# Triangular inverse in a delta-rule and RWKV mixer: from a substitution on VectorE to doublings on TensorE

## The chip, the cores and the metric

The kernel runs on one NeuronCore of one Trainium2 chip, in one launch. The metric is the device time of that launch in microseconds (us), lower is better. Five engines work in parallel, each in its own program order: TensorE (PE in the profile, its weight loads PEld), VectorE (DVE), ScalarE (ACT), GpSimd (POOL) and the DMA queues that SyncE (SP) issues to.

## What is computed

Three residual blocks follow one another on 512 tokens of 1024 channels. The change lies in the third. There a gated delta rule and an RWKV-7 layer run over the tokens in four chunks of 128, for eight heads each. Inside a chunk the state update needs the solution of a unit lower triangular system, 128 by 128, for each head and chunk. The reference solves it per head and chunk; in the kernel's form it is

```
Y = ((I + L)^-1)^T        L: strictly lower triangular, 128 x 128, float32
u = Y^T r                 r: 128 tokens x 64 channels
```

The kernel computes Y for two heads and four chunks at a time, so one call of `tri_inv` inverts 8 matrices, and there are 8 calls: four for the RWKV layer (`rwkv_b`), four for the delta rule (`gdn_b`).

## The kernel before

Channels lie on partitions and tokens on the free axis, except inside the mixers, where tokens lie on partitions. All large projections are matmuls of 128 by 128 weights on 512 tokens. Each weight unit is loaded by SP, rounded to a high part on ACT (L310) and completed by a low part on DVE (L312), and `mm3` (L325 to L327) issues three matmuls for each 128 channels of contraction. The order of instructions on every engine is set by a scheduler at build time; the list `MIX3` and the offsets in `PR3` say in which order and with which priority the steps of the mixers are handed to it: `ra`, `rb`, `rd` prepare, invert and run the RWKV layer of two heads, `ga`, `gb`, `gd` the delta rule. On chip each engine takes its instructions in that fixed order and waits for semaphores.

`tri_inv` (L1740) works on the four diagonal blocks of 32 of each matrix, which lie on four groups of 32 partitions:

- ACT copies the negated blocks into `iv_lc` (L1750); DVE transposes them into `iv_ld` (L1753).
- Blocks of 16 are inverted by substitution on DVE, one row at a time, all 8 matrices and both 16-blocks together: 15 steps of a product (L1756) and a sum over it (L1757), each waiting for the one before.
- Two more transposes on DVE (L1759, L1761) give the inverse in both orientations, `iv_xc` and `iv_yc`.
- 16 to 32: 32 small matmuls of 32 by 32 (L1769), a copy to SBUF on ACT (L1771), 32 and 24 more matmuls (L1775, L1778), and two additions on DVE (L1780, L1781).
- 32 to 64 (L1790 to L1801) and 64 to 128 (L1806 to L1812) go on in the same manner on TensorE and ACT.

The matmuls of `tri_inv` write to the PSUM banks of the use `mx`, of which there are two; `rwkv_b` (L2046), `gdn_b` (L1877, L1886) use the same two.

## Time and profile before

| | us |
|---|---|
| median of 3 runs (lowest, highest) | 3515.52 (3511.62, 3516.84) |
| span of the profiled execution, first to last instruction | 3510.5 |
| PE busy in the span | 3380.7 |
| DVE busy in the span | 2413.4 |
| ACT busy in the span | 1802.1 |

The profiled execution is one execution; its own time shown is the span, 5.0 us below the median of the runs. The stage in which the 8 inversions lie goes from about 2544 us to 2998 us after the span's start. All positions below are us from the span's start. [...] A float32 matmul stands in the trace as two records, one instruction of the program.

### The profile page before, as it was taken

The numbers are of one execution on the slowest core, as the hardware profiler recorded it, in microseconds if no ns is written. First come the engines' busy times: TensorE is split into PE (matmuls) and PEld (weight loads), VectorE is DVE, ScalarE is ACT, GpSimd is POOL, SyncE is SP. The second block draws the span as 40 slices with busy tenths as digits, with TensorE's granted clock in tenths as the row PEclk, the third lists the DMA queues.
The fourth block names the chain that finished last, engine by engine and source line by source line (L and its number), as shares of the span: only waits on it lengthen the run. The fifth ranks groups of instructions, "written<-read, shape, count | busy, mean of one in ns | idle before, by whom it ended". The sixth has DMA issues, their size and how long they took to land.

```text
span 3510.5 us, 50868 instructions
## 1 busy us (share of the span) xinstructions
PE 3380.7 (96%) x20328; PEld 2686.3 (77%) x20328; DVE 2413.4 (69%) x3883; ACT 1802.1 (51%) x3000; POOL 123.6 (4%) x56
## 2 busy tenths in 40 slices
PE   7999999999799999999999999999899999999998
PEld 5888888888577777766787778888667667878887
DVE  6787767787689988466565465554757788565545
ACT  6556556466544565444455543334636556544434
POOL 0000000000132330000000000000000000000000
PEclk9999999999899999999999999999969999999999
DMA  6233323321121122333321235542201111323332
GB/s 224 88 102 95 100 91 100 106 79 55 49 72 61 66 78 95 123 108 108 93 79 58 86 120 180 186 157 96 102 21 45 34 43 37 105 88 96 96 96 84
DMA packets 109663, 325.10 MB, mean 93 GB/s; under 512 B 12721, under 2 KB 13361, under 8 KB 108786
## 3 DMA queue, kind: packets, MB, share of 16 engines
q1 hardware_dynamic: 109170, 321.06, 28.1%
q8 instruction: 160, 2.62, 0.3%
q0 software_dynamic: 256, 0.79, 0.1%
q14 instruction: 77, 0.63, 0.1%
HBM read 315.51 MB, written 6.29 MB: 92 GB/s over the span
## 4 chain that ended last, share of the span: by engine, by line
PE 78%; DVE 15%; ACT 4%; issue 2%; DMA 2%; POOL 0%; SPq 0%; DVEq 0%; ACTq 0%
PE ps_pj L326 19%; PE ps_pj L325 19%; PE ps_pj L327 19%; DVE w_lo L312 2%; DMA ada_raw<-ada_w 2%; DVE iv_m L1756 1%; PE ps_mx L1388 1%; PE ps_pj L1365 1%; PE ps_mx L2046 1%; PE ps_o L1394 1%; ACT w_hi L310 1%; DVE iv_xd L1757 1%; PE ps_ad L496 1%; PE ps_mx L326 1%; DVE cv_ul L318 1%
## 5 line engine op out<-in xcount | busy, mean ns | idle before, releaser
L325 PE MATMUL ps_pj<-hh,w_hi 128*128 128x512 f32 x2344 | 937.4, 401 | 19.8 <-ACT hh L397 18.9
L327 PE MATMUL ps_pj<-hh,w_lo 128*128 128x512 f32 x2344 | 935.0, 399 | 0.0
L326 PE MATMUL ps_pj<-hl,w_hi 128*128 128x512 f32 x2344 | 934.9, 399 | 0.0
L310 ACT CAST w_hi<-w_raw 128x1024 fp32r<-128x1024 f32 (+1 forms) x435 | 454.6, 1045 | 767.4 <-PE ps_pj L326 651.2
L312 DVE TENSOR_TENSOR w_lo<-w_raw,w_hi 128x1024 fp32r<-128x1024 f32 (+1 forms) x387 | 470.2, 1216 | 336.4 <-ACT w_hi L310 330.3
L325 PEld LDWEIGHTS ps_pj<-hh,w_hi 128*128 128x128 f32 x2344 | 445.9, 190 | 127.5 <-ACT hh L397 24.3
L326 PEld LDWEIGHTS ps_pj<-hl,w_hi 128*128 128x128 f32 x2344 | 446.0, 190 | 102.0 <-issue 12.9
L327 PEld LDWEIGHTS ps_pj<-hh,w_lo 128*128 128x128 f32 x2344 | 445.6, 190 | 101.3 <-issue 10.7
L493 DVE SCALAR_TENSOR_TENSOR ada_acc<-ada_raw,sv_t_c,ada_acc 128x512 f32<-128x512 f32 x224 | 167.4, 747 | 50.3 <-DMA ada_raw<-ada_w 48.5
L967 DVE SCALAR_TENSOR_TENSOR xT<-ps_pj,ad,xT 128x512 f32<-128x512 f32 x128 | 95.5, 749 | 153.8 <-PE ps_pj L327 153.3
L312 POOL TENSOR_TENSOR w_lo<-w_raw,w_hi 128x1024 fp32r<-128x1024 f32 x48 | 121.1, 2523 | 1175.5 <-ACT w_hi L310 1175.5
L909 DVE SCALAR_TENSOR_TENSOR ps_mx<-cv_ut,vec,ps_mx 128x448 f32<-128x448 f32 (+3 forms) x192 | 128.3, 669 | 1.9 <-PE ps_mx L327 1.0
L909 DVE SCALAR_TENSOR_TENSOR ps_ad<-cv_ut,vec,ps_ad 128x480 f32<-128x480 f32 (+2 forms) x192 | 128.5, 669 | 1.6 <-ACT ps_ad L898 0.5
L327 PE MATMUL ps_pj<-w_hi,hl 128*128 128x256 f32 x416 | 119.0, 288 | 2.5 <-DVE hl L398 2.5
L325 PE MATMUL ps_pj<-w_hi,hh 128*128 128x256 f32 x416 | 120.3, 290 | 0.8 <-ACT hh L397 0.6
L326 PE MATMUL ps_pj<-w_lo,hh 128*128 128x256 f32 x416 | 120.8, 291 | 0.0
L326 PE MATMUL ps_pj<-m_yl,w_hi 128*128 128x512 f32 x256 | 99.9, 390 | 0.0
L327 PE MATMUL ps_pj<-m_yh,w_lo 128*128 128x512 f32 x256 | 99.6, 389 | 0.0
L325 PE MATMUL ps_pj<-m_yh,w_hi 128*128 128x512 f32 x256 | 99.6, 389 | 0.0
L327 PEld LDWEIGHTS ps_pj<-w_hi,hl 128*128 128x128 f32 x416 | 80.7, 195 | 5.7 <-DVE hl L398 3.2
L325 PEld LDWEIGHTS ps_pj<-w_hi,hh 128*128 128x128 f32 x416 | 80.9, 194 | 3.6 <-ACT hh L397 1.2
L326 PEld LDWEIGHTS ps_pj<-w_lo,hh 128*128 128x128 f32 x416 | 80.8, 194 | 1.5 <-issue 0.7
(786 smaller groups left out, 6513.4 us busy)
## 6 DMA issues: line engine op xcount, KB each, us to landing
ada_raw<-ada_w SPq DMA_DIRECT2D x288, 256.0 KB, 2.8
w_raw<-w_in SPq DMA_DIRECT2D x97, 512.0 KB, 3.2
w_raw<-hgrn_w_in SPq DMA_DIRECT2D x64, 512.0 KB, 3.2
w_raw<-w_mlp SPq DMA_DIRECT2D x64, 512.0 KB, 3.3
w_raw<-conv_w_in SPq DMA_DIRECT2D x48, 512.0 KB, 3.2
w_raw<-w_ffn_in SPq DMA_DIRECT2D x44, 512.0 KB, 3.5
w_raw<-hgrn_w_v SPq DMA_DIRECT2D x16, 512.0 KB, 3.3
w_raw<-hgrn_w_out SPq DMA_DIRECT2D x16, 512.0 KB, 3.2
```

Of the source, the lines that this page charges most:

```text
L310: nc.scalar.copy(hi, raw)
L312: (nc.gpsimd if self.on_pool else nc.vector).tensor_tensor(lo, raw, hi.bitcast(F32), op=ALU.subtract)
L318: self.nc.vector.tensor_tensor(lo, src, hi.bitcast(F32), op=ALU.subtract)
L325: mm(out, wh, xh, start=first, stop=False)
L326: mm(out, wh, xl, start=False, stop=False)
L327: mm(out, wl, xh, start=False, stop=last)
L493: nc.vector.scalar_tensor_tensor(acc, raw, cond[:, k:k + 1], acc, op0=ALU.mult, op1=ALU.add)
L496: nc.tensor.matmul(col[:, b:b + 1], acc[:, 128 * b:128 * b + 128], self.c("ones")[:, 0:1], start=True, stop=True)
L909: stt(o, x, tap(j), o, op0=ALU.mult, op1=ALU.add)
L967: self.nc.vector.scalar_tensor_tensor(self.xT[:, m, :], acc, gate[:, m:m + 1], self.xT[:, m, :], op0=ALU.mult, op1=ALU.add)
L1365: mm(sc[:, :n], q[gs, 128 * i:n], ks[b][gs, 0:n], start=True, stop=True)
L1388: mm(banks[c // 512][:, c % 512:c % 512 + 128], p_[:, off[i] + 128 * s:off[i] + 128 * s + 128], dg[:, i, :], start=True, stop=True)
```

## The change

The substitution, its three transposes and the separate step from 16 to 32 go. In their place the diagonal blocks grow from 2 to 32 in four equal levels (2 to 4, 4 to 8, 8 to 16, 16 to 32). One product on DVE cuts the blocks into five masked parts, one for each level (`iv_c`, 128 x 1280); the first part plus the identity is the inverse of the blocks of 2. Each level is 32 matmuls, a copy on ACT, 64 matmuls and one addition on DVE of both orientations (`iv_xy`, 128 x 512). From 32 to 128 nothing changes. The constant `m16` becomes `mlev` and `eye32`, so one constant load grows from 128x160 to 128x320 elements. Comments are stripped from the file, which shifts line numbers; the cuts below are the code.

```diff
-    b3 = {"bones": ..., "m16": f((p % 32 < 16) & (np.arange(32)[None] >= 16))}
+    s32, t32 = p % 32, np.arange(32)[None]
+    lev = [(s32 // (2 * w) == t32 // (2 * w)) & (s32 % (2 * w) < w) & (t32 % (2 * w) >= w) for w in (1, 2, 4, 8, 16)]
+    b3 = {"bones": ..., "mlev": -f(np.concatenate(lev, axis=1)), "eye32": f(s32 == t32)}
...
         for q in q4:
-            nc.scalar.mul(lc[q, 0:8, :], LA[q, :, 0, q], -1.0)
-        ld = iv("iv_ld")
-        nc.vector.transpose(ld.rearrange("p t s -> p t s"), lc.rearrange("p h t -> p t h"))
-        for i in range(1, 16):
-            m = self.tmpd("iv_m", [P, 2, i, i])
-            tt(m, dview(ld, 32 * i, [[528, 2], [0, i], [1, i]]), dview(xd, 0, [[528, 2], [1, i], [32, i]]), op=ALU.mult)
-            nc.vector.tensor_reduce(dview(xd, 32 * i, [[528, 2], [1, i]]), m, axis=mybir.AxisListType.X, op=ALU.add)
-        nc.vector.transpose(xc.rearrange("p h j -> p j h"), xd.rearrange("p i j -> p j i"))
-        nc.vector.transpose(yc.rearrange("p h i -> p i h"), xd)
-        tt(c16, lc[:, 0:8, :], self.c("m16").unsqueeze(1).to_broadcast([P, 8, 32]), op=ALU.mult)
-        (one level: 32 matmuls, copy, 32 + 24 matmuls, two additions)
+            nc.scalar.copy(lc[q], LA[q, :, 0, q])
+        tt(cl, lc.unsqueeze(1).to_broadcast([P, 5, 8, 32]),
+           self.c("mlev").rearrange("p (l t) -> p l t", l=5).unsqueeze(2).to_broadcast([P, 5, 8, 32]), op=ALU.mult)
+        tt(xy[:, 1], cl[:, 0], b8(self.c("eye32")), op=ALU.add)
+        nc.vector.transpose(xy[:, 0].rearrange("p h t -> p (h t)"), xy[:, 1].rearrange("p h t -> p (h t)"))
+        for lev in range(1, 5):
+            ps = self.bank("mx", [P, 8, 32])
+            for hc in range(8):
+                for q in q4:
+                    mm(ps[q, hc, :], cl[q, lev, hc, :], xx[q, hc, :], start=True, stop=True)
+            b = c32("iv_b")
+            nc.scalar.copy(b, ps)
+            ps = self.bank("mx", [P, 2, 8, 32])
+            for hc in range(8):
+                for q in q4:
+                    mm(ps[q, 1, hc, :], b[q, hc, :], yy[q, hc, :], start=True, stop=True)
+                for q in q4:
+                    mm(ps[q, 0, hc, :], yy[q, hc, :], b[q, hc, :], start=True, stop=True)
+            tt(xy, xy, ps, op=ALU.add)
```

The scheduler places the rest anew around these instructions, from the first inversion on; the set of all other instructions stays. TensorE before, at the second inversion: the last projections that stand ahead of it, then its one level from 16 to 32 (L1769, L1775, L1778) and the next step (L1790).

```order
L325 MATMUL ps_pj<-hh,w_hi 128x512
L326 MATMUL ps_pj<-hl,w_hi 128x512
L327 MATMUL ps_pj<-hh,w_lo 128x512
L325 MATMUL ps_pj<-hh,w_hi 128x512
L1769 MATMUL ps_mx<-iv_xc,iv_b 32x32 x32
L326 MATMUL ps_pj<-hl,w_hi 128x512
L1819 MATMUL ps_pa<-rw_sq,cst_b_20722 128x512
L1775 MATMUL ps_mx<-iv_yc,iv_b 32x32 x32
L1778 MATMUL ps_mx<-iv_b,iv_yc 32x32 x24
L1977 MATMUL ps_pa<-s_lo,rw_lw 128x512
```

TensorE now, at the second inversion: the end of its first level's 64 matmuls (L1774 and L1776 alternate in fours, eight times), what is put in before the second level (L1768), its 32 matmuls, and what is put in before the next 64. L328 to L330 are the three matmuls of `mm3`, L2025 is the second matmul of the RWKV layer's gate.

```order
L1776 MATMUL ps_mx<-iv_b,iv_xy 32x32 x4
L2025 MATMUL ps_pa<-s_sg_20780,rw_lw 128x512
L330 MATMUL ps_pj<-hh,w_lo 128x512
L328 MATMUL ps_pj<-hh,w_hi 128x512
L329 MATMUL ps_pj<-hl,w_hi 128x512
L1768 MATMUL ps_mx<-iv_xy,iv_c 32x32 x32
L330 MATMUL ps_pj<-hh,w_lo 128x512
L328 MATMUL ps_pj<-hh,w_hi 128x512
L329 MATMUL ps_pj<-hl,w_hi 128x512
L330 MATMUL ps_pj<-hh,w_lo 128x512
L328 MATMUL ps_pj<-hh,w_hi 128x512
L1774 MATMUL ps_mx<-iv_xy,iv_b 32x32 x4
```

Between the levels stand one to five matmuls of other work in most places; the run of 17 projections that stood ahead of the second inversion before is spread over these gaps. DVE before, at the end of the second inversion's substitution: a step of it stands between two instructions of other work, and the two transposes follow.

```order
L1756 TENSOR_TENSOR iv_m<-iv_ld,iv_xd 128x450
L1493 TENSOR_TENSOR gd_gz<-gd_gz,si_e 128x512
L1757 TENSOR_REDUCE iv_xd<-iv_m 128x2x15
L1642 SCALAR_TENSOR_TENSOR rw_k<-rw_pad,s_mu_20735,rw_k 128x512
L1759 STREAM_TRANSPOSE iv_xc<-iv_xd 128x32x32
L1761 STREAM_TRANSPOSE iv_yc<-iv_xd 128x32x32
L312 TENSOR_TENSOR w_lo<-w_raw,w_hi 128x1024 x2
```

DVE now, at the second inversion: the additions that end its first two levels (L1777) and what stands between and behind them. L437, L1496 and L1853 are work of the delta rule's preparation, L315 is the low part of a weight.

```order
L1777 TENSOR_TENSOR iv_xy<-iv_xy,ps_mx 128x512
L437 SCALAR_TENSOR_TENSOR si_e<-gd_z,si_e 128x512
L1853 SCALAR_TENSOR_TENSOR gd_z<-gd_pad,vec_20708,gd_z 128x512
L1496 TENSOR_TENSOR gd_z<-gd_z,si_e 128x512
L1637 MEMSET rw_pad 128x1
L437 SCALAR_TENSOR_TENSOR si_e<-gd_z,si_e 128x512
L315 TENSOR_TENSOR w_lo<-w_raw,w_hi 128x1024
L1777 TENSOR_TENSOR iv_xy<-iv_xy,ps_mx 128x512
```

Where 15 pairs of short instructions stood, one inversion now has four additions, each behind other work in the queue.

## Rows read from the trace of the kernel before

**Rows 1.** The page: busy us of each engine, share of the span, instructions.

```profile
PE 3380.7 (96%) x20328; PEld 2686.3 (77%) x20328; DVE 2413.4 (69%) x3883; ACT 1802.1 (51%) x3000; POOL 123.6 (4%) x56
```

**Rows 2.** Busy time by stretch (start:end, length, engines), granted clock, DMA: the whole stage.

```profile
core 0: us, PE busy (x) PEld busy (x) DVE busy (x) ACT busy (x) POOL busy (x), PEclk, DMA share, GB/s
2544.00:2998.00 454.00, 427.65 (x3920) 314.04 (x3919) 344.22 (x695) 254.04 (x509) 1.61 (x3) 0.90 0.11 37
```

**Rows 3.** The stage's critical chain by line, shares of its 454 us.

```profile
by line: DVE iv_m L1756 9.2%; PE ps_mx L2046 8.1%; DVE iv_xd L1757 6.0%; PE ps_pj L327 5.2%; PE ps_pj L326 5.0%; PE ps_pj L325 4.6%; DVE w_lo L312 3.6%; PE ps_mx L1886 3.5%; DVE iv_xc L1759 3.3%; DVE iv_yc L1761 2.8%; issue 2.7%; PE ps_mx L
```

**Rows 4.** Waits of TensorE in the stage: us in total, times, longest.

```profile
PE ps_mx L1769 <- DVE iv_xc L1759: 8.7, 7, 2.3
PE ps_pa L1830 <- DVE rw_B L2013: 4.6, 1, 4.6
PE ps_mx L1778 <- issue: 2.2, 4, 0.9
```

**Rows 5.** Groups of DVE in the stage: form, count, busy us, mean ns, idle before.

```profile
L1756 DVE TENSOR_TENSOR iv_m<-iv_ld,iv_xd 128x2 f32<-128x2 f32 (+14 forms) x120 | 55.4, 461 | 1.9
L1757 DVE TENSOR_REDUCE iv_xd<-iv_m 128x2 f32<-128x2 f32 (+14 forms) x120 | 38.8, 324 | 1.8
L312 DVE TENSOR_TENSOR w_lo<-w_raw,w_hi 128x1024 fp32r<-128x1024 f32 x30 | 36.5, 1218 | 8.2 <-ACT w_hi L310 8.2
L1759 DVE STREAM_TRANSPOSE iv_xc<-iv_xd 128x1024 f32<-128x1024 f32 x8 | 16.7, 2082 | 0.0
L1753 DVE STREAM_TRANSPOSE iv_ld<-iv_lc 128x1024 f32<-128x1024 f32 x8 | 15.7, 1967 | 1.7 <-ACT iv_lc L1750 1.7
L1761 DVE STREAM_TRANSPOSE iv_yc<-iv_xd 128x1024 f32<-128x1024 f32 x8 | 15.6, 1948 | 0.0
L1780 DVE TENSOR_TENSOR iv_yy<-iv_yc,ps_mx 128x256 f32<-128x256 f32 x8 | 3.4, 420 | 0.0
L2025 DVE TENSOR_TENSOR rw_bon<-rw_v,ps_pa 128x512 f32<-128x512 f32 x4 | 2.8, 688 | 1.4 <-PE ps_pa L2024 1.4
```

**Rows 6.** TensorE at the second inversion, full clock: start, us, records, idle before.

```profile
2667.55 0.75 PE L1769 MATMUL ps_mx<-iv_xc,iv_b 32*32 32x32 f32 x64 [2.28 <-DVE iv_xc L1759]
2668.23 0.50 PE L326 MATMUL ps_pj<-hl,w_hi 128*128 128x512 f32 x1
2669.53 0.72 PE L1775 MATMUL ps_mx<-iv_yc,iv_b 32*32 32x32 f32 x62
2670.10 0.67 PE L1778 MATMUL ps_mx<-iv_b,iv_yc 32*32 32x32 f32 x46
2670.70 1.12 PE L1977 MATMUL ps_pa<-s_lo,rw_lw 64*128 64x512 f32 x2
2672.92 0.69 PE L1790 MATMUL ps_mx<-iv_xx,s 32*32 32x32 f32 x32 [0.66 <-DVE iv_xx L1781]
```

**Rows 7.** DVE just behind that level, and ACT's copy at the third inversion.

```profile
2672.04 0.41 DVE L1780 TENSOR_TENSOR iv_yy<-iv_yc,ps_mx 128x256 f32<-128x256 f32 x1
2724.67 0.37 ACT L1771 COPY iv_b<-ps_mx 128x256 f32<-128x256 f32 x1 [1.77 <-PE ps_mx L1769]
```

**Rows 8.** TensorE at the first inversion, where the clock was low.

```profile
2584.37 1.07 PE L1775 MATMUL ps_mx<-iv_yc,iv_b 32*32 32x32 f32 x64 [0.18 <-DVE iv_yc L1761]
2586.15 1.06 PE L1778 MATMUL ps_mx<-iv_b,iv_yc 32*32 32x32 f32 x47 [0.69 <-issue]
2587.14 0.80 PE L327 MATMUL ps_pj<-hh,w_lo 128*128 128x512 f32 x1
```

**Rows 9.** Busy time and clock of the stage in four stretches, columns as in rows 2.

```profile
2540.00:2565.00 25.00, 24.31 (x56) 15.48 (x57) 14.78 (x35) 6.32 (x14) 0.54 (x1) 0.50 0.07 23
2565.00:2583.00 18.00, 16.58 (x111) 11.06 (x112) 14.62 (x22) 9.75 (x14) 0.00 (x0) 0.94 0.10 36
2583.00:2642.00 59.00, 57.45 (x407) 41.62 (x396) 29.31 (x53) 21.61 (x48) 0.00 (x0) 0.54 0.06 19
2642.00:2998.00 356.00, 332.62 (x3378) 248.41 (x3378) 288.09 (x593) 219.82 (x440) 1.07 (x2) 0.99 0.13 42
```

## The prediction

> **What bounds the kernel now.** The page comes first: TensorE is busy 96% of the span, DVE 69%, ACT 51% [rows 1]. Whatever adds TensorE work that nothing hides costs time; what it takes from DVE pays only where TensorE waits for DVE. All 8 inversions lie in one stage, so the busy time of that stretch was read next: in 454.0 us TensorE is busy 427.65 (94%) and idle 26.4, DVE is busy 344.2 (76%) [rows 2].

> The third view, the stage's critical chain, says something else at first sight. The substitution and its transposes (L1756, L1757, L1759, L1761) hold 9.2 + 6.0 + 3.3 + 2.8 = 21.3% of it, 97 us, more than any matmul [rows 3]. It is no promise of 97 us. The chain is followed back from whoever came last, and while it runs along DVE, TensorE works off projections that stand ahead of the inversion. What DVE's lateness costs is TensorE's idle time, and the list of its waits sizes it: 8.7 us before L1769 for `iv_xc`, 4.6 us before L1830 for `rw_B`, which DVE made late because steps of a substitution stood between its own steps, and 2.2 us without a releaser in L1778 [rows 4]. That is 15.5 us of the 26.4.

> **Taken from DVE.** Per group: 55.4 (L1756) + 38.8 (L1757) + 16.7 + 15.7 + 15.6 (three transposes of 1024 columns), and three small additions and products of which one row stands, 3.4 and twice 3.3. Together 152.2 us, 19.0 per inversion [rows 5].

> **Added on DVE,** per inversion: the masked product of 1280 columns, 1.52 us from L312's 1024 columns in 1218 ns; the sum with the identity at L1780's 0.42; a transpose of 256 columns, 0.49 as a quarter of L1761 (between 0.42 and the full 1.95); four additions of 512 columns from PSUM at L2025's 0.688, so 2.75 [rows 5]. Together 5.2, or 41 us over 8, and DVE is 111 us freer. That pays nothing by itself; it removes the 15.5 us of waits. Bounds: nothing of them (the waits come back elsewhere) to all 26.4; I take 15.5. ACT's three further copies, 3 x 0.37 us [rows 7], make 9 us over 8 inversions in an engine that is busy 254 of 454 us [rows 2]: nothing, as long as they aren't late.

> **Added on TensorE.** Before, an inversion had 32 + 32 + 24 = 88 matmuls of 32 by 32 in this part, now 4 x (32 + 64) = 384. The price is taken from start to next start, since the durations overlap. L1769's 32 start at 2667.55, the next matmul at 2668.23: 0.68 us. L1775 starts at 2669.53, L1778 at about 2670.10, and L1977 at 2670.70: 0.57 us for 32 and 0.60 for 24 [rows 6]. So 1.85 us per inversion go. A new level has 0.68 for its first 32; its next 64 are 32 of L1775's kind and 32 of L1778's, 0.57 + 0.60 x 32/24 = 1.37. That is 2.05 a level, 8.2 an inversion, net 6.35, and 51 us over 8. Lower bound: all 64 at L1775's pace, 4 x (0.68 + 1.14) - 1.85 = 5.4, or 43 us. Upper bound: the pace under the low clock throughout, where L1775 takes 0.85 us (2584.37 to the first L1778, as its 1.07 less the overlap) and L1778 0.99 for 47 records (2586.15 to 2587.14) [rows 8]: 4 x (0.85 + 0.85 + 0.99 x 64/47) - 1.85 = 10.34, or 83 us. I take 51, since the stretch after 2642 has a granted clock of 0.99 [rows 9] and holds seven inversions.

> [...]

> **New waits.** The DVE chain is replaced by exchanges: after each 32 matmuls TensorE needs ACT's copy, after each 64 DVE's addition, 8 per inversion, 64 in all. The copy is 0.37 us and starts at once behind L1769's end [rows 7], the addition 0.69. In the new order each gap holds one to ten matmuls of other work, mostly 0.7 to 1.6 us of them by my count, an estimate, so an exchange that is served at once is hidden. It costs where the queue is late. Behind L1778's end at 2670.77, L1780 started only at 2672.04, behind other DVE work, and TensorE then idled 0.66 us before L1790 although L1977 and a projection had been put between [rows 6, 7]. In the new order w_lo (1.22 us) and the delta rule's 512-column operations stand ahead of many additions just so. I charge 0.66 to each of the 32 gaps that wait for DVE, none to those that wait for ACT: 21 us. Bounds: 0, if fillers always cover; 32 x (1.22 + 0.69) = 61 us if each addition comes behind one w_lo and nothing covers. Behind a waiting matmul stand projections whose results feed ACT and DVE, so such a wait delays them too; with TensorE the bound, that is not counted twice.

> **The clock.** From 2540 to 2565 the granted clock is 0.50, in the 18 us of projections up to 2583 it recovers to 0.94, and from 2583 to 2642 it is 0.54, though TensorE is busy 57.45 of 59 us there, with small float32 matmuls and few projections [rows 9]. In the new order the first inversion stands right behind the float32 scores of `rb0`, without the long run of projections. So the 16.6 us of TensorE work in 2565 to 2583 may run at the lower level too, and the first inversion's levels at the pace of rows 8. Bounds 0 and 16.6 + 4; I take 10.

> **Sum.** -15.5 + 51 + 21 + 10 = +66 us, on the span of 3510.5: 3577. The runs shown lie 5.0 us higher in the median, so the forecast for the changed kernel is 3582 us. A change that stays hidden is excluded by the floor: 427.65 + 51 us of TensorE work do not fit into 454 at the same clock.

> **Rivals.**

> - *The clock falls in every inversion* (18%). [...] For: it was at 0.50 to 0.54 in 84 us of the stage, once it had waited [rows 9]. [...] Price: levels at the slow pace, 83 - 51 = 32 us, and some 8 us of other work in each of seven inversions at half speed, an estimate, less the 21 us of waits that this hides: 32 + 56 - 21 = +67, so 3649 us. [...] Rows 9 show the falls, but no run here yet shows them from bursts alone.
> - *The exchanges are bare* (12%). Both DVE and ACT serve late: +61 in place of +21, 3622 us. For: L1790's wait [rows 6]. Against: DVE is 111 us freer.
> - *Cheaper than charged* (12%). All 64 matmuls of a level at L1775's pace, no new waits, no clock loss: 43 - 15.5 = +27, so 3543 us.
> - *Faster* (6%). The stage is paced by DVE after all, as the chain has it: 97 us leave the chain, 41 come back, 3460 us. It decides for this if TensorE's busy time, whose ends are modelled, hides more than the 51 us of idle that the bursts need. Against: the projections' regular starts at full clock around L1769.
> - *It evens out* (3%). With the waits gone the clock stays up from 2540 to 2642: 84 us at about half give back some 40, so 51 - 15.5 - 40 = -4, within 0.2%.

> The forecast's own band, 3555 to 3610, has 49%. Of the rest, the low end 3530 leaves out 9% and the high end 3640 about 11%, most of the clock's case; so the range is 3530 to 3640. About 0.2%, 7 us, is what a measurement of this kernel can tell from no change: slower 90%, same 4%, faster 6%.

> **What the profile after would show.** Right: DVE's busy time lower by about 110 us; the waits of L1769 for `iv_xc` and of L1830 for `rw_B` gone; each new burst of 32 about 0.7 us and of 64 about 1.4 us to the next start; TensorE's idle time in the stage no smaller than before, now split into many waits below 1 us in front of L1768 and L1774; the stage longer by 60 to 70 us and everything outside it unchanged. Wrong: bursts dearer or cheaper than that; a granted clock well under 0.99 behind the first two inversions, or near 1.0 in the first; or a shorter stage with TensorE's busy time lower, which would mean that its busy time before was waiting in disguise.

## The result and the profile after

The changed kernel takes 3559.8 us in the median of 4 runs (3556.88 to 3561.57), the kernel before 3516.18 beside it: a ratio of 1.0121, 95% interval [1.0096, 1.0146]. It is slower, by 44 us where 66 were forecast. The profiled execution took 3556.88 us, its span is 3555.1. In the changed file the lines that matter are `mm3` at L328 to L330, the copies to `iv_lc` at L1753, `iv_c` at L1756, the first sum and transpose at L1760 and L1761, the 32 matmuls of a level at L1768, the copy to `iv_b` at L1770, the 64 matmuls at L1774 and L1776, the addition at L1777, and the step from 32 to 64 at L1786.

The page of the kernel after, busy time of each engine (beside [rows 1]):

```profile
PE 3415.2 (96%) x25064; PEld 2717.9 (76%) x25064; DVE 2318.7 (65%) x3648; ACT 1812.2 (51%) x3024; POOL 123.6 (3%) x56
```

The executions are then cut at 2540 and at 440 us before the end, so that the stage with the inversions begins and ends at the same place of the program in each. First the stage of the kernel before by this cut (columns as in [rows 2]):

```profile
2540.00:3070.50 530.50, 501.98 (x4267) 374.69 (x4268) 387.34 (x768) 290.75 (x566) 1.61 (x3) 0.91 0.14 48
3070.50:3510.50 440.00, 425.58 (x1841) 346.06 (x1839) 240.76 (x296) 190.87 (x264) 0.00 (x0) 0.99 0.30 92
```

And of the kernel after:

```profile
2540.00:3115.10 575.10, 537.34 (x9011) 408.47 (x9012) 295.70 (x537) 301.69 (x590) 1.62 (x3) 0.96 0.14 44
3115.10:3555.10 440.00, 425.59 (x1837) 345.75 (x1835) 239.85 (x294) 190.87 (x264) 0.00 (x0) 0.98 0.30 92
```

The difference of the spans, 44.6 us, lies in the stage alone (575.1 less 530.5). TensorE is busy 35.4 us longer there and idle 9.2 us longer (37.8 after, 28.5 before), the granted clock (PEclk, the share of full clock that TensorE was given) is higher (0.96 for 0.91), and DVE is busy 91.6 us less. The idle time grew by these 9 us only, but most of it is now ended by something else. The waits of TensorE in the stage after (beside [rows 4]):

```profile
PE ps_mx L1776 <- issue: 16.3, 16, 1.8
PE ps_mx L1768 <- issue: 9.0, 11, 1.6
PE ps_mx L1774 <- issue: 7.5, 5, 1.8
PE ps_pj L328 <- DVE s L437: 1.5, 1, 1.5
PE ps_mx L1786 <- issue: 0.9, 1, 0.9
PE ps_o L2063 <- issue: 0.9, 1, 0.9
PE ps_mx L1768 <- DVE iv_xy L1777: 0.8, 2, 0.4
```

The waits for `iv_xc` and `rw_B` are gone. The exchanges, which the forecast charged with 21 us, cost 0.8. In their place stand 34.6 us, in 34 waits, that no semaphore ends ("issue"). A stretch of TensorE's timeline (start, us, engine, line, records, idle time before) shows four of them:

```profile
2918.29 0.75 PE L1768 MATMUL ps_mx<-iv_xy,iv_c 32*32 32x32 f32 x64 [0.36 <-issue]
...
2921.76 0.22 PE L1776 MATMUL ps_mx<-iv_b,iv_xy 32*32 32x32 f32 x2 [1.17 <-issue]
...
2925.23 0.26 PE L1768 MATMUL ps_mx<-iv_xy,iv_c 32*32 32x32 f32 x7 [0.96 <-issue]
...
2928.70 0.21 PE L1774 MATMUL ps_mx<-iv_xy,iv_b 32*32 32x32 f32 x2 [1.51 <-issue]
```

They are 3.47 us apart, three times in a row, and by the trace exactly 128 matmul records lie between two of them. They fall in the middle of a burst as often as at its head: at 2925.23 with 57 of L1768's 64 records done. An exchange, whose waits stand at a burst's head, doesn't do that. Of the stage's 38 idle gaps over 0.25 us, 34 lie on one such grid: counted from one to the next, 128 records or a multiple of it, at most 3 short (a few records are missing from a trace). The queue that the profile calls "instruction" (q8) grew in step; packets, MB and share in the stage, first of the kernel before:

```profile
q8 instruction: 33, 0.54, 0.4%
```

and after:

```profile
q8 instruction: 70, 1.15, 0.8%
```

The stage holds 4744 matmul records and 4744 weight loads more than before (9011 less 4267, 9012 less 4268), 9488 instructions, and 37 packets of this queue more, read here as fetches of the program: 256 instructions to a fetch of 16.4 KB (1.15 MB by 70). An instruction is here a record: 128 records of matmuls, which are 64 float32 matmuls, and 128 weight loads. That is the distance of the stops.

The packets of this queue stand in front of the stops' ends in the trace. Each of the 34 on the grid ends 1.26 to 1.58 us after the end of a packet of q8, which takes 0.88 to 1.47 us. At the last three shown above the packet began 1.13 to 1.14 us after the group before had begun, and not sooner. All the added burst's stops in the next section end in the same way, 1.21 to 1.58 us behind a packet.

### The profile page after: what moved, and what is told of

Same layout as the page of the kernel before. It is cut to its first block, busy times and chain, and to the rows that moved or that the text cites. A ratio compares the mean times of both kernels' runs of the same rounds, so it can differ in the third digit from the quotient of the medians.

```text
span 3555.1 us, 60144 instructions
## 1 busy us (share of the span) xinstructions
PE 3415.2 (96%) x25064; PEld 2717.9 (76%) x25064; DVE 2318.7 (65%) x3648; ACT 1812.2 (51%) x3024; POOL 123.6 (3%) x56
## 4 chain that ended last, share of the span: by engine, by line
PE 83%; DVE 10%; ACT 3%; issue 3%; DMA 1%; POOL 0%; SPq 0%; DVEq 0%; ACTq 0%
PE ps_pj L328 20%; PE ps_pj L330 20%; PE ps_pj L329 20%; DVE w_lo L315 1%; PE ps_mx L1391 1%; PE ps_pj L1368 1%; PE ps_o L1397 1%; PE ps_mx L2042 1%; PE ps_mx L329 1%; PE ps_ad L499 1%; DVE cv_ul L321 1%; ACT w_hi L313 1%; PE ps_mx L1768 1%; PE ps_mx L726 1%; DMA ada_raw<-ada_w 1%
## 5 line engine op out<-in xcount | busy, mean ns | idle before, releaser
L328 PE MATMUL ps_pj<-hh,w_hi 128*128 128x512 f32 x2344 | 938.7, 401 | 18.9 <-ACT hh L400 18.9
L330 PE MATMUL ps_pj<-hh,w_lo 128*128 128x512 f32 x2344 | 936.2, 400 | 1.0 <-DVE w_lo L315 0.6
L315 DVE TENSOR_TENSOR w_lo<-w_raw,w_hi 128x1024 fp32r<-128x1024 f32 (+1 forms) x387 | 470.5, 1217 | 400.4 <-ACT w_hi L313 376.1
L328 PEld LDWEIGHTS ps_pj<-hh,w_hi 128*128 128x128 f32 x2344 | 446.9, 191 | 122.3 <-ACT hh L400 24.5
L330 PEld LDWEIGHTS ps_pj<-hh,w_lo 128*128 128x128 f32 x2344 | 446.0, 190 | 100.0 <-issue 8.4
L315 POOL TENSOR_TENSOR w_lo<-w_raw,w_hi 128x1024 fp32r<-128x1024 f32 x48 | 121.1, 2523 | 1175.5 <-ACT w_hi L313 1175.5
L330 PE MATMUL ps_pj<-w_hi,hl 128*128 128x256 f32 x416 | 119.0, 288 | 2.5 <-DVE hl L401 2.5
L328 PE MATMUL ps_pj<-w_hi,hh 128*128 128x256 f32 x416 | 120.3, 290 | 0.8 <-ACT hh L400 0.7
L330 PE MATMUL ps_pj<-m_yh,w_lo 128*128 128x512 f32 x256 | 99.6, 389 | 0.0
L328 PE MATMUL ps_pj<-m_yh,w_hi 128*128 128x512 f32 x256 | 99.6, 389 | 0.0
L330 PEld LDWEIGHTS ps_pj<-w_hi,hl 128*128 128x128 f32 x416 | 80.6, 195 | 5.7 <-DVE hl L401 3.2
L328 PEld LDWEIGHTS ps_pj<-w_hi,hh 128*128 128x128 f32 x416 | 80.8, 194 | 3.7 <-ACT hh L400 1.4
```

The lines of the kernel that those rows point to most:

```text
L315: (nc.gpsimd if self.on_pool else nc.vector).tensor_tensor(lo, raw, hi.bitcast(F32), op=ALU.subtract)
L328: mm(out, wh, xh, start=first, stop=False)
L330: mm(out, wl, xh, start=False, stop=last)
```

## The experiments

**Theory A** was formed from this: TensorE's program reaches it 256 instructions at a time, one block follows another no sooner than after some 3.5 us, and small matmuls use up 128 records with their weight loads sooner than that; the stops, not the exchanges, are what the new levels add to their own pace. **Rival B** is the prediction's: waits between levels, or the bursts' pace alone. Each ratio below is to the kernel before, run beside.

**A long run of small matmuls by itself.** Into the kernel before, 288 independent matmuls of 32 by 32 per inversion, which wait for no result of one another and which nobody waits for.

```diff
+        ps2 = self.bank("mx", [P, 8, 32])
+        for k in range(9):
+            for hc in range(8):
+                for q in q4:
+                    mm(ps2[q, hc, :], yc[q, hc, :], xc[q, hc, :], start=True, stop=True)
         yy, xx = c32("iv_yy"), c32("iv_xx")
```

> The kernel before with 288 more matmuls of 32 by 32 in each inversion, in one run, behind its one level; they read tiles that are ready and nobody reads their bank, so the output doesn't change and no exchange with ACT or DVE is added. Theory A (instruction supply): every 256 instructions of TensorE come in one 16 KB fetch, a run of small matmuls uses them up faster than they come, and it stops once per fetch. Then the run shows idle stretches without a releaser, about 1.5 to 2 us at every 128th record, and the time is 8 x 288 x 22.5 ns = 52 us of work plus 8 x 3.5 stops x 2 us = 56 us, near 3620 us. Theory B (the new waits of the change are its exchanges with ACT and DVE): a run without exchanges has no stops, 52 us, near 3568 us.

Measured: 3697.22 us, ratio 1.0502 [1.0454, 1.0550]. Stage, waits, and the burst of the second inversion in the timeline (the added matmuls are L1783):

```profile
2540.00:3267.10 727.10, 638.87 (x8865) 489.80 (x8864) 389.59 (x762) 289.57 (x558) 1.61 (x3) 0.74 0.10 35
```

```profile
PE ps_mx L1783 <- issue: 63.3, 33, 3.2
```

```profile
2682.91 1.93 PE L1783 MATMUL ps_mx<-iv_xc,iv_yc 32*32 32x32 f32 x128 [2.18 <-issue]
2686.66 1.93 PE L1783 MATMUL ps_mx<-iv_xc,iv_yc 32*32 32x32 f32 x128 [1.82 <-issue]
2690.41 1.93 PE L1783 MATMUL ps_mx<-iv_xc,iv_yc 32*32 32x32 f32 x128 [1.82 <-issue]
```

This is Theory A undisguised: groups of exactly 128 records, 1.93 us of work each, one every 3.75 us, and 33 stops with no exchange in sight. What neither side expected is the clock, 0.74 over the stage, and with it a time 77 us above A's 3620: beyond the 63 us of stops and the burst's own 52 (2304 matmuls at the 22.5 ns of the levels, see the next section), TensorE was busy 85 us longer, some 73 of it on other work (from start to next start, less idle time).

**As many instructions, twice the columns.** The same burst with 64 moving columns.

```diff
-        ps2 = self.bank("mx", [P, 8, 32])
+        ps2 = self.bank("mx", [P, 8, 64])
...
-                    mm(ps2[q, hc, :], yc[q, hc, :], xc[q, hc, :], start=True, stop=True)
+                    mm(ps2[q, hc, :], yc[q, hc, :], xc[q, hc:hc + 2, :].rearrange("p a b -> p (a b)"), start=True, stop=True)
```

> The kernel of e1_burst_alone with 64 moving columns in place of 32 in each of the 288 added matmuls of an inversion: as many instructions, twice the columns. Theory A, that the supply of instructions sets the pace of a long run of small matmuls: the stops shrink from 66 us to under 20 and the busy time grows by as much, and the time stays within 20 us of e1's 3697. [...]

Measured: 3640.48 us, ratio 1.0353 [1.0316, 1.0390]. Stage, and the burst of the second inversion:

```profile
2540.00:3178.20 638.20, 565.81 (x8863) 442.92 (x8862) 389.23 (x761) 289.92 (x558) 1.62 (x3) 0.92 0.12 40
```

```profile
2656.58 3.00 PE L1783 MATMUL ps_mx<-iv_xc,iv_yc 32*32 32x64 f32 x128 [2.10 <-issue]
2660.05 2.29 PE L1783 MATMUL ps_mx<-iv_xc,iv_yc 32*32 32x64 f32 x128 [0.47 <-issue]
2663.53 1.99 PE L1783 MATMUL ps_mx<-iv_xc,iv_yc 32*32 32x64 f32 x128 [1.18 <-issue]
2667.28 1.99 PE L1783 MATMUL ps_mx<-iv_xc,iv_yc 32*32 32x64 f32 x128 [1.76 <-issue]
```

The groups again begin 3.47 to 3.75 us apart, and where a group is longer the stop behind it is shorter. From the first to the last start a burst takes 14.8 to 19.4 us (mean 16.5) with 64 columns and 15.1 to 20.2 (mean 16.6) with 32: twice the columns did not change the pace. The expected size was off: the stops fell from 63.3 to 49.5 us, not below 20. And the run is 57 us faster than the one with half the columns, at a clock of 0.92 in place of 0.74; nobody expected that either, and no run shows why.

**Only the last level.** The kernel after with levels 1 to 3 left out, so that the inverse lacks them.

```diff
-        for lev in range(1, 5):
+        for lev in range(4, 5):
```

> The changed kernel with only the last of its four levels (levels 1 to 3 are left out: 288 matmuls, three copies and three additions per inversion, so the inverse is not the right one). TensorE then has about the work of before (96 against 88 small matmuls per inversion) and DVE has none of the substitution: what the freed DVE gives by itself. By the prediction's terms (15.5 us of waits, no gain from the clock): 3501 us. If all idle time of the stage and the low clock's loss go with the substitution, as the profile of the changed kernel has it: 26 + 24 us, 3466 us. If the stage was paced by DVE: below 3450 us.

Measured: 3452.4 us, ratio 0.9812 [0.9789, 0.9834].

```profile
2540.00:3014.30 474.30, 464.09 (x4407) 357.47 (x4406) 280.83 (x514) 290.24 (x569) 1.61 (x3) 0.97 0.16 53
```

This kernel has 768 small matmuls where the kernel before has 704, and its stage is 56.2 us shorter: 18.3 us of idle time (28.5 to 10.2) and 37.9 of busy time, most of which is the clock (an estimate by stretches of 10 us: 14.8 us lost to it in place of 46.0). So what leaves DVE, with the new order that this brings, is worth 56 us, not the 15.5 of the forecast; and the three added levels then cost 101 us (575.1 less 474.3).

**The second orientation by DVE.** The kernel after with half of the 64 matmuls replaced by a transpose of 256 columns. It takes 32 matmuls from each level and adds a wait to it.

```diff
-            ps = self.bank("mx", [P, 2, 8, 32])
+            ps = self.bank("mx", [P, 8, 32])
             for hc in range(8):
                 for q in q4:
-                    mm(ps[q, 1, hc, :], b[q, hc, :], yy[q, hc, :], start=True, stop=True)
-                for q in q4:
-                    mm(ps[q, 0, hc, :], yy[q, hc, :], b[q, hc, :], start=True, stop=True)
-            tt(xy, xy, ps, op=ALU.add)
+                    mm(ps[q, hc, :], b[q, hc, :], yy[q, hc, :], start=True, stop=True)
+            tt(yy, yy, ps, op=ALU.add)
+            nc.vector.transpose(xx.rearrange("p h t -> p (h t)"), yy.rearrange("p h t -> p (h t)"))
```

> The changed kernel with the second orientation made by DVE: after each level's addition on 256 columns a transpose of 256 columns in place of 32 matmuls, the same inverse. 128 matmuls per inversion less on TensorE, one DVE operation more in each exchange. Theory A: 8 x 128 x 22.5 ns = 23 us of work go, and with 256 instructions a level in place of 384 most of the 35 us of stops, so near 3508 us. Theory B: the work goes and the exchanges get longer by 0.44 us each, 32 x 0.44 = 14, near 3550 us.

Measured: 3492.93 us, ratio 0.9927 [0.9907, 0.9948]. Stage, and its largest wait:

```profile
2540.00:3050.40 510.40, 501.32 (x6960) 378.88 (x6961) 297.61 (x565) 299.19 (x588) 1.61 (x3) 0.98 0.15 50
```

```profile
PE ps_mx L1774 <- issue: 4.4, 4, 1.4
```

Theory A holds, B falls: a third fewer small matmuls, and the stops nearly vanish (TensorE is idle 9.1 us of the stage) although each level has one more DVE operation between its matmuls and the next level's. This version is faster than both kernels.

**Levels that don't wait for one another.** The kernel after; each level reads the starting `xy`, its addition goes to another tile, so the dependence between levels is left out.

```diff
+        xs = self.tmpd("iv_xs", [P, 2, 8, 32])
...
-            tt(xy, xy, ps, op=ALU.add)
+            tt(xs, xy if lev == 1 else xs, ps, op=ALU.add)
+        xx, yy = xs[:, 0], xs[:, 1]
```

> The changed kernel with levels that don't wait for one another: each reads the inverse of the blocks of 2 and adds to one sum (the dependence between levels is left out, so the inverse is not the right one). Same instructions, no wait of a level for the addition before it. Theory A: the stops without a releaser stay, 30 us or more, and the time stays within 10 us of 3560. Theory B: the waits go and the time falls by about 30 us, to 3530.

Measured: 3578.52 us, ratio 1.0170 [1.0144, 1.0196].

```profile
2540.00:3142.60 602.60, 557.14 (x9004) 431.65 (x9003) 296.35 (x531) 297.78 (x586) 1.62 (x3) 0.89 0.13 43
```

```profile
PE ps_mx L1769 <- issue: 20.1, 10, 4.1
PE ps_mx L1777 <- issue: 10.6, 12, 1.6
PE ps_mx L1775 <- issue: 10.1, 10, 1.4
```

With the waits between levels out of the way the stops are still there, 41 us, and the kernel is no faster but slower, at a clock of 0.89. B falls here too; A has the stops right, but the time lies 19 us above 3560 where it allowed 10.

**Where do the 56 us come from?** Six runs asked whether it is DVE's load, the inversion's path, or the order of the projections. Three are the faster version above with a chain of maxima of a tile with itself on DVE.

```diff
+        s = self.tmpd("iv_s", [P, 8, 32])
+        nc.vector.tensor_copy(s, lc)
+        for i in range(34):
+            tt(s, s, s, op=ALU.max)
```

In the first, nobody reads `s`.

> The kernel of e3_x_by_transpose with, in each of the eight inversions, a chain of one copy and 34 element-wise maxima of 128x256 on DVE (34 x about 0.41 us, some 14 us), whose result nobody reads; the output stays the reference's. It gives DVE back about 114 us of work (more than the 95 us that the change took from it), but not on the path of an inversion. What is disputed is where the 56 us come from that the run with one doubling level gained over its own price: (P) from the path, because the inversion's first matmuls no longer stand behind a long DVE chain: then this run stays near 3493, at most 3505, with an idle TensorE of about 9 us in the stage at a clock of 0.98. (L) from DVE's load, because evictions that TensorE waits for came late behind the chain: then it goes back by most of the gain, to about 3540, with idle time of some 25 us and the clock below 0.93. (O) from the other order of the projections' matmuls: then it stays near 3493 here and in e6_load_on_path.

Measured: 3486.85 us, ratio 0.9922 [0.9900, 0.9944].

```profile
2540.00:3050.90 510.90, 501.69 (x6967) 378.46 (x6968) 390.85 (x853) 299.21 (x594) 1.62 (x3) 0.98 0.16 51
```

DVE is busy 390.9 us of the stage, more than in the kernel before (387.3), and nothing is lost: TensorE is idle 9.2 us, 9.1 without the chain. L falls.

In the second, `iv_c` is computed from `s`.

> The same chain as in e5_load_off_path, but the scaled coefficients are computed from its result, so each inversion's first matmul waits for it; the output stays the reference's. (P) about 3540: idle time of TensorE in the stage back at some 25 us and the clock at 0.91 to 0.93, as in the kernel before. (L) the same as e5_load_off_path, about 3540 in both. (O) about 3493 in both, because the matmuls of the projections fill the wait.

Measured: 3619.03 us, ratio 1.0292 [1.0270, 1.0315].

```profile
2540.00:3179.40 639.40, 579.07 (x6961) 434.01 (x6962) 399.97 (x853) 305.42 (x595) 1.62 (x3) 0.83 0.12 40
```

TensorE's idle time is 60.3 us and the clock 0.83: P holds, O falls, but the loss is 126 us, not 47. From the first copy to `iv_lc` to the last write of an inversion it now takes 64.8 us on average, against 34.6 without the chain and 46.9 in the kernel before, so the path is longer than the one it was to imitate. Hence a run with half the chain (`range(17)`):

> The kernel of e6_load_on_path with 17 maxima in place of 34 in each inversion's chain (some 7 us); the output stays the reference's. An inversion from its first copy to its last write took 34.6 us on average in e3_x_by_transpose, 64.8 in e6_load_on_path and 46.9 in the kernel before. Theory P2, that the stage pays for each us of an inversion's length: length some 50 us, and a time between the two in proportion, 3493 + (50 - 34.6) / (64.8 - 34.6) x 126 = 3557, with the clock near 0.91 and 25 to 35 us of idle time. Rival T, that other work of TensorE covers an inversion up to about the length that it had before, and only what is longer is paid: 3500 to 3515, with the clock at 0.96 or more.

Measured: 3502.75 us, ratio 0.9959 [0.9943, 0.9974].

```profile
2540.00:3066.90 526.90, 512.12 (x6968) 385.85 (x6969) 351.10 (x717) 301.91 (x594) 1.62 (x3) 0.96 0.15 50
```

An inversion of 49.7 us costs 10 us only: cover up to a length, and a price beyond it (T), not a price for every us (P2). That left the kernel before unexplained, whose inversions are shorter than these. The last three runs took this up. Two keep the kernel before and change the scheduler's priority of the inversions. The number says how many instructions earlier than they stand the steps are handed over, so with 200 they go ahead of less other work and with 600 of more.

```diff
-PR3 = {"a": 0, "b": 400, "d": 500, "s": 300, "p": 150, "t": 300, "u": 0}
+PR3 = {"a": 0, "b": 200, "d": 500, "s": 300, "p": 150, "t": 300, "u": 0}
```

> The kernel before, with the substitution, and the priority number of block 3's inversions lowered from 400 to 200: the scheduler puts the same instructions in another order around the inversions. It asks what is left of the gain that a freed DVE brought, since neither DVE's load nor an inversion of 50 us brought the loss back. Theory O, that the loss of the kernel before is one of its order (some 9 us of waits in front of L1769 and one fall of the clock behind the first inversion that lasts 59 us): the order changes the idle time and the clock of the stage, and the time moves by 10 to 40 us in one of these two runs, down where the first inversion's wait is covered. Rival S, that the substitution's own chain of 30 short steps costs it in any order: both runs within 10 us of 3515, clock 0.90 to 0.92 and 25 us or more of idle time.

> As e10_before_priority_200, with the number raised from 400 to 600: the inversions' steps go ahead of more other work. Theory O: a move by 10 to 40 us in one of the two runs, up where less work is left to cover the first inversion's wait. Rival S: within 10 us of 3515, clock 0.90 to 0.92 and 25 us or more of idle time.

Measured: with 200, 3539.99 us, ratio 1.0061 [1.0037, 1.0085]; with 600, 3524.73 us, ratio 1.0016 [0.9995, 1.0036], which can't be told from no change. The profiled execution with 600 took 3511.69 us, 13 us less than the median. Stage and first wait with 200:

```profile
2540.00:3094.80 554.80, 519.40 (x4275) 390.48 (x4276) 393.37 (x771) 293.83 (x568) 1.62 (x3) 0.88 0.14 46
```

```profile
PE ps_mx L1769 <- DVE iv_xc L1759: 10.3, 7, 3.3
```

and with 600:

```profile
2540.00:3069.80 529.80, 498.86 (x4271) 373.67 (x4272) 387.22 (x770) 292.48 (x568) 1.62 (x3) 0.91 0.15 48
```

```profile
PE ps_mx L1769 <- DVE iv_xc L1759: 8.3, 8, 2.3
```

Rival S as it was put, within 10 us of 3515 in any order, falls with the first run: one order costs 22 us. Of O that much holds, but neither of the other orders gains. L1769 waits 8.3 to 10.3 us in all three, and the clock is 0.88 to 0.91. So the order is a part of the price, and whether the substitution as such is another stayed open.

The last one puts a chain of maxima in front of the one-level kernel: the wait comes in one piece, as in the substitution, with one level behind it. As in that kernel, three levels are left out; the diff is against it.

```diff
+        s = self.tmpd("iv_s", [P, 8, 32])
+        nc.vector.tensor_copy(s, lc)
+        for i in range(38):
+            tt(s, s, s, op=ALU.max)
...
-        tt(cl, lc.unsqueeze(1).to_broadcast([P, 5, 8, 32]),
+        tt(cl, s.unsqueeze(1).to_broadcast([P, 5, 8, 32]),
```

> The kernel of e2_one_level (the last doubling alone, the first three left out, so that its output isn't the reference's) with a chain of one copy and 38 maxima on DVE ahead of the scaled coefficients, some 16 us in each inversion: the substitution's load and its place on the path, in front of one level, but not its arithmetic, its short operands or its wide transposes. e2_one_level took 3452.4 us, the kernel before 3516. Theory P3, that a long wait in one piece, with one level behind it, is what cost the kernel before its idle time and its clock, whatever DVE computes in it: 3500 to 3525, with 25 us or more of idle time and a clock of 0.90 to 0.93. Rival S, that it is a property of the substitution itself: below 3475, clock 0.95 or more, as e9_half_load_on_path came out.

Measured: 3549.01 us, ratio 1.0097 [1.0075, 1.0119].

```profile
2540.00:3107.00 567.00, 512.10 (x4398) 385.43 (x4397) 385.64 (x823) 291.56 (x565) 1.62 (x3) 0.88 0.13 44
```

Idle time 54.9 us, clock 0.88: a long wait of quite other DVE work costs too, 97 us over the kernel without the chain. S falls, and P3 holds in kind; its time, 3500 to 3525, was missed by 24 us, with a wait longer than the substitution's. Two things keep it from being the whole account of the kernel before. The first small matmuls (L1772) themselves wait 10.6 us of the 54.9; the rest lies at other places, the largest part in front of projections (L328):

```profile
PE ps_pj L328 <- ACT gd_pad L1846: 8.1, 3, 4.4
PE ps_mx L1772 <- DVE iv_xy L1765: 5.4, 1, 5.4
PE ps_mx L1772 <- DVE gd_pad L1845: 5.2, 1, 5.2
```

And the clock falls elsewhere: in the stretches of [rows 9] it is 0.64, 1.00, 0.97 and 0.86 here, where the kernel before had 0.50, 0.94, 0.54 and 0.99. The table sets the wait, from the start of the first copy to `iv_lc` to the start of the first small matmul, mean and extremes of the eight inversions, beside what the stage paid.

| kernel | first copy to first small matmul, us | stage, us | TensorE idle, us | clock | time, us |
|---|---|---|---|---|---|
| one level, no chain | 6.9 (4.7 to 10.1) | 474.3 | 10.2 | 0.97 | 3452.4 |
| before (one level, substitution) | 30.3 (21.2 to 45.6) | 530.5 | 28.5 | 0.91 | 3516.2 |
| before, priority 200 | 29.3 (24.1 to 32.7) | 554.8 | 35.4 | 0.88 | 3540.0 |
| before, priority 600 | 31.0 (23.7 to 46.5) | 529.8 | 30.9 | 0.91 | 3524.7 |
| one level, chain of 38 | 41.5 (37.5 to 50.7) | 567.0 | 54.9 | 0.88 | 3549.0 |
| four levels with transposes | 7.8 (5.4 to 12.8) | 510.4 | 9.1 | 0.98 | 3492.9 |
| the same, chain of 17 | 21.2 (17.2 to 29.0) | 526.9 | 14.8 | 0.96 | 3502.8 |
| the same, chain of 34 | 38.5 (34.6 to 43.6) | 639.4 | 60.3 | 0.83 | 3619.0 |

From the first row to the second it is 64 us of time for 23.4 us of mean wait, and from there to the chain of 38 it is 33 for 11.2: 2.7 and 2.9 us for each. That is no rule. The kernel before with priority 200 waits 1 us less than with 400 and takes 22 us more, and with four levels the first 13.4 us of wait cost 10 us and the next 17.3 cost 116. The length of the wait and the order around it both count, and no run separates them.

One run only looked for a better version: the one with transposes, priority 200. Its expectation has the direction the wrong way round: with 200 an inversion's steps go ahead of less other work.

> The kernel of e3_x_by_transpose with the priority number of block 3's inversions lowered from 400 to 200, so that the scheduler emits an inversion's steps ahead of more of the projections' work. It is tried as a better version. If the waits for DVE and ACT between an inversion's steps are covered by what stands between them on TensorE, fewer projections lie there and the idle time rises over e3's 9 us: 3495 to 3515. If they are not what costs, the time stays within 5 us of 3493.

Measured: 3496.28 us, ratio 0.9947 [0.9925, 0.9968]; no better than with 400, and TensorE is idle 13.5 us in its stage where it was 9.1.

## Why the prediction was right, and where it was not

The direction was right, and the time came out inside the range partly by luck: only one of the four terms was right, and the errors of the others nearly cancelled. The stage's balance, of 44.6 us:

| term | forecast, us | measured, us | from |
|---|---|---|---|
| waits for other engines that go | -15.5 | -23 | idle time without "issue": 28.5 - 2.2 before, 37.8 - 34.6 after |
| pace of the bursts | +51 | +51 | start to next start less idle time: 69.2 us for 3072 matmuls, 18.3 for 704 |
| waits of the exchanges | +21 | +0.8 | L1768 behind L1777; it lies in the 3.2 us above |
| stops without a releaser | none | +32 | 34.6 after, 2.2 before |
| clock | +10 | about -20 | (1 - granted clock) x length, an estimate summed over stretches of 10 us: 46.0 us lost before, 25.7 after |
| rest | none | about +5 | 44.6 less the others |

**Bursts, right.** 69.2 by 3072 is 22.5 ns a matmul of two records. Both halves came out some 3.5 us above the forecast (8 x 8.2 = 65.6 for the new bursts, 8 x 1.85 = 14.8 for the old), so the difference is nearer than the prices were. The whole prediction stands on this term, and it was read from starts in [rows 6], not from durations.

**Exchanges, wrong as a cause.** The step that failed is "I charge 0.66 to each of the 32 gaps that wait for DVE". L1790's wait in [rows 6] was one case, and the scheduler's fillers cover nearly every other. The amount came back as something else: stops that no semaphore ends, 128 records or a multiple of it apart and each ended 1.26 to 1.58 us behind a packet of q8. Their first sign stood in [rows 4], L1778's four waits "without a releaser", which the prediction counted among the waits that DVE's relief removes. A wait with no releaser needed a cause of its own. Here it was 2.2 us with runs of 56 small matmuls between other work, and it grew to 34.6 with four times as many in a row of levels.

The trace puts a block at 256 instructions (9488 instructions, 37 fetches), and in runs of small matmuls its end was not hidden: 0.34 to 1.78 us were lost at each of the 34 stops of the kernel after, and 1.82 to 2.18 at the three shown of the burst run. Had the ends been hidden, the 32 us in the table would be near nothing.

**Freed DVE, mis-sized, and the clock, of the wrong sign.** Together the forecast gave -15.5 + 10, and the run with one level puts them at -56. The step that failed is that DVE's relief "removes the 15.5 us of waits" and nothing more: of the 56 us, 18.3 are idle time and some 31 are clock. In the kernel before the clock was 0.54 from 2583 to 2642, behind the first inversion [rows 9]. The kernel after, in the same four stretches as [rows 9]:

```profile
2540.00:2565.00 25.00, 24.79 (x370) 17.72 (x372) 11.40 (x20) 7.13 (x16) 0.54 (x1) 0.66 0.03 7
2565.00:2583.00 18.00, 14.80 (x531) 9.94 (x521) 6.00 (x9) 10.46 (x20) 0.00 (x0) 0.81 0.03 7
2583.00:2642.00 59.00, 54.22 (x1035) 39.35 (x1034) 39.18 (x66) 35.22 (x72) 0.54 (x1) 1.00 0.10 32
2642.00:3032.00 390.00, 361.89 (x6718) 274.38 (x6718) 196.62 (x376) 208.73 (x425) 0.54 (x1) 0.96 0.11 36
```

The clock is 1.00 where it was 0.54, although TensorE is idle 4.8 us there. That is what the rival "It evens out" supposed, with 3% and 40 us: of clock some 29 us came back up to 2642 (an estimate from these rows) and some 9 were lost behind it, beside costs that the rival didn't have. What in the earlier order makes the clock stay low for 59 us of nearly unbroken work is not shown by any run.

**DVE's busy time** fell by 91.6 us in the stage, not 111. The durations did fall by 111.0 (all DVE records of the stage add up to 431.0 us before and 320.1 after), but records overlap, and busy time counts an overlap once. The 240 short steps don't overlap one another, 94.2 us either way; they overlap the other work that stands between them, by 20.6 us. The price of the new DVE work was right; its groups after (columns as in [rows 5]):

```profile
L1777 DVE TENSOR_TENSOR iv_xy<-iv_xy,ps_mx 128x512 f32<-128x512 f32 x32 | 22.0, 686 | 56.2 <-PE ps_mx L1776 56.2
L1756 DVE TENSOR_TENSOR iv_c<-iv_lc,cst_b 128x1280 f32<-128x1280 f32 x8 | 11.9, 1488 | 5.3 <-ACT iv_lc L1753 5.3
L1761 DVE STREAM_TRANSPOSE iv_xy<-iv_xy 128x256 f32<-128x256 f32 x8 | 3.5, 441 | 0.1
```

**The rivals.** "The clock falls in every inversion" did not happen here (0.96), but a run with small matmuls and stops between them had such falls: 0.74 over the stage with 288 bare matmuls per inversion. "The exchanges are bare" fell with the exchange term. "Cheaper than charged" was right that the exchanges cost next to nothing, but the bursts were no cheaper, and it had no stops. "Faster", a stage paced by DVE, was wrong as put, since DVE's load alone cost nothing (3486.85 us with 93 us more of it, 3492.93 without); but the substitution that the chain showed was worth 56 us of its 97, and with a third fewer small matmuls the change is a gain of 0.7%.

**What stays open.** The rest of about 5 us lies in busy time, and no run shows its cause. Not separated either are the parts that the length of the wait, the order of the other work and the substitution's own form have in the 56 us. The runs show that a long DVE chain on the path cost that much and more (97 us with one level and 38 maxima, 126 with four levels and 34), and that DVE's load off the path cost nothing (3486.85 us for 3492.93).

## What to carry to other kernels

Count instructions, not only columns, when work moves to TensorE as many small matmuls: here, in long runs of them, every 256 took 3.47 to 3.75 us in the stretches shown, and a float32 matmul is four (two records and two weight loads), so 32 matmuls saved in each level by a transpose of 0.44 us on a less busy engine turned a loss of 1.2% into a gain of 0.7%. A wait that the trace ends with no releaser was a resource of its own here (2.2 us before, 34.6 after), and should be priced as one before it is multiplied by four. What a freed engine was worth here was not its load but the long piece of the path that TensorE's other work didn't cover; that piece's price included the clock that was lost with it (an estimated 31 of the 56 us), and it changed with the order of the other work (22 us between priorities 200 and 400).
